# The last merge-gate units as Strassen pairs, and three helper chains cut into steps on VectorE's queue

## The chip, the cores and the metric

The kernel runs on one core of a Trainium2 chip. The number judged is the device time of one execution, in microseconds, the median over the runs of a kernel. Before the change it is 1549.16 us, the median of three runs that lie between 1545.98 and 1551.1 us. A separate execution was taken with the profiler; its own time was 1545.69 us and its span, from the first to the last recorded instruction, 1543.9 us.

The engines are TensorE (PE in the profile, with its weight loads as PEld), VectorE (DVE), ScalarE (ACT), GpSimd (POOL) and SyncE (SP), which here issues nearly all DMA transfers.

## What is computed

An encoder block over 1024 tokens of width 1024. A normalised input `h` is multiplied by one wide matrix; three attention branches (A, dilated windows in three groups; B, grouped-query; M, cross-attention into a memory) produce `oa`, `ob` and `om`, each 512 wide. What matters here is the end of it:

```python
h = rms_norm(x, g_pre[layer])
a_qkv, bq, bk, bv, mq, ga, gb, gm, mg = jnp.split(h @ w_in[layer], split_at, axis=-1)
...
wts = jax.nn.softmax(jnp.stack(lses, axis=0), axis=0).astype(dt)
oa = jnp.einsum('gbsh,gbshd->bshd', wts, jnp.stack(outs, axis=0)).reshape(b, s, BRANCH_WIDTH)
...
ya = (oa * jax.nn.silu(ga)) @ w_br_a[layer]
yb = (ob * jax.nn.silu(gb)) @ w_br_b[layer]
ym = (om * jax.nn.silu(gm)) @ w_br_m[layer]
gates = jax.nn.sigmoid((mg + b_merge[layer]).astype(jnp.float32)).astype(dt).reshape(b, s, N_BRANCHES, d)
merged = gates[:, :, 0] * ya + gates[:, :, 1] * yb + gates[:, :, 2] * ym
out = merged @ w_out[layer]
x = x + rms_norm(out, g_post[layer])
```

The merge gates `mg` are 3072 columns of the wide product: 24 units of 128 columns, each a product of 1024 x 128 weights with 1024 x 1024 of `h`.

## The kernel before

Everything is held transposed, channels on the 128 partitions and tokens along the row. Every float32 operand is split in two parts of a shorter type, high and low (`split`, lines 104 to 106: ScalarE copies to the high part, VectorE subtracts it to get the low part), and a product is three passes: high with high, high with low, low with high. `hh[k]` and `hl[k]` are the parts of `h`, k from 0 to 7.

`dense` (lines 139 to 148) does one half (512 tokens) of a unit of 128 output columns: 8 values of k times 3 passes, 24 matmuls of 128x512. A unit is 48 matmuls. `add_unit` queues such units with a function that takes each half out of PSUM; `weave` interleaves the queue's matmuls with an attention's, by costs. TensorE runs in the order written; the other engines' queues are ordered when the program is built, by a scheduler that looks at priorities and at when it thinks operands are there. A queue is strictly in order once built: what waits at its head holds up all behind it.

The stages, in the order of time: start and memory projection; branch M; branch B; branch A with twelve attentions (four pairs of heads p_, three groups g); the merge; the output projection. Ten of the 24 merge-gate units are computed early, as fillers during B and A (`add_filler`, `FILL_B`, `FILL_A`): the eviction multiplies by the row `rb` on VectorE (line 212), ScalarE does the tanh, and the result goes out to DRAM (`thd`).

`combine(p_, ogs)` (lines 1042 to 1072) is the softmax over the three groups of one pair of heads. It reads the statistics back, makes three weights per token on small tiles, writes them out, and then for each group and each half loads them broadcast over the partitions (`wgt`, line 1065, one buffer), multiplies (line 1069, VectorE, 128x512, read with a stride) and adds the groups on GpSimd (line 1071). For p_ = 0, 1, 2 it stands between two attentions; for p_ = 3 in the merge, behind the first branch's operands.

The merge (lines 1094 to 1192) goes over the branches in the order 2, 1, 0 and over eight column blocks f. `mg_unit` computes one merge gate (48 matmuls, for the 14 units that were not spilled) or loads it from `thd`; `y_unit` computes one block of a branch's product (24 matmuls), multiplies it by the gate on VectorE and adds it into `accs[f]` on GpSimd (line 1128). The gate runs two steps ahead of the product. A branch's operand is `od[i]` times its silu gate `g2d[i]` (and a normaliser for branch 1), split in parts; `g_load` fetches and multiplies, all of it in one place half way through the branch before. After the last product the eight weight tiles of the output projection are loaded and split (lines 1198 to 1203), and eight token blocks are projected, normalised and stored.

Of the kernel before, what the change touches and what calls it, by code (L numbers as in the profile page):

```python
# [8 lines left out]
F32 = mybir.dt.float32  # L9
R = mybir.dt.float32r  # L10
# [6 lines left out]
NT = 8  # L17
# [33 lines left out]
def block(ctx: ExitStack, tc: tile.TileContext, x, xT, memT, cst, msk, bcst, tabA, gpost,  # L51
# [757 lines left out]
    with tc.tile_pool(name="aa", bufs=1, reuse_waits="tile") as aa:  # L809
# [81 lines left out]
        def a_att(p_, g):  # L891
# [29 lines left out]
            st = {}  # L921
# [5 lines left out]
            def scores(T):  # L927
# [6 lines left out]
                for h in range(2):  # L934
# [4 lines left out]
                    V.tensor_tensor_reduce(raw, sv[:, h], mask[:, mo:mo + n], 1.0, 3.0e38, OP.add, OP.min, bias)  # L939
# [102 lines left out]
        def combine(p_, ogs):  # L1042
            cpt = cb.tile([P, 3, 2, 16], F32, name="cpt", bufs=1)
            for h in range(2):
                nc.sync.dma_start(cpt[h * 64:h * 64 + 64], std[p_, h].rearrange("g s (i e) -> i g s e", e=16))
            mn = cb.tile([P, 16], F32, name="cmn", bufs=2)
            V.tensor_tensor(mn, cpt[:, 0, 0], cpt[:, 1, 0], op=OP.min)
            V.tensor_tensor(mn, mn, cpt[:, 2, 0], op=OP.min)
            eg = cb.tile([P, 3, 16], F32, name="ceg", bufs=1)
            V.tensor_tensor(eg, cpt[:, :, 0], mn[:, None, :].to_broadcast([P, 3, 16]), op=OP.subtract)  # L1050
            A.activation(eg, eg, AF.Exp, scale=-1.0)
            dn = cb.tile([P, 3, 16], F32, name="cdn", bufs=1)
            V.tensor_tensor(dn, eg, cpt[:, :, 1], op=OP.mult)
            ds_ = cb.tile([P, 16], F32, name="cds", bufs=2)
            V.tensor_tensor(ds_, dn[:, 0], dn[:, 1], op=OP.add)
            V.tensor_tensor(ds_, ds_, dn[:, 2], op=OP.add)
            V.reciprocal(ds_, ds_)
            V.tensor_tensor(eg, eg, ds_[:, None, :].to_broadcast([P, 3, 16]), op=OP.mult)
            for h in range(2):
                nc.sync.dma_start(wgd[p_, h].rearrange("g (i e) -> i g e", e=16), eg[h * 64:h * 64 + 64])  # L1060
            for g in range(3):
                for e in range(2):
                    wgt = cb.tile([P, 512], F32, name="wgt", bufs=1)
                    for h in range(2):
                        nc.sync.dma_start(wgt[h * 64:h * 64 + 64],
                                          wgd[p_, h, g:g + 1, e * 512:e * 512 + 512].to_broadcast([64, 512]))
                    wv = wgt.rearrange("p (b a) -> p a b", b=8)
                    ogv = ogs[g].rearrange("p (a b) -> p a b", b=16)[:, :, e * 8:e * 8 + 8]
                    V.tensor_tensor(ogv, ogv, wv, op=OP.mult)
                if g:  # L1070
                    G.tensor_tensor(ogs[0], ogs[0], ogs[g], op=OP.add)
            nc.sync.dma_start(od[0, p_], ogs[0])

        seq = [(p_, g) for p_ in range(4) for g in range(3)]
# [3 lines left out]
        for n, (p_, g) in enumerate(seq):  # L1078
# [9 lines left out]
            if g == 2 and p_ < 3:  # L1088
                combine(p_, [OG.pop((p_, x)) for x in range(3)])

    end_psum()
# [3 lines left out]
    with tc.tile_pool(name="mg", bufs=1, reuse_waits="tile") as mg:  # L1095
        accs = [None] * 8
        extra.extend((mg, wp))

        def mg_unit(i, f):
            th = mg.tile([P, S], F32, name="th", bufs=3)  # L1100
            if 8 * i + f in spilled:
                nc.sync.dma_start(th, thd[8 * i + f])
                return th
            w = load_w(wu[U_M + 8 * i + f])
            s = pss()
            for half in range(2):
                for _ in dense(w, half, s[:, half]):
                    pass
            V.tensor_tensor(th, s.rearrange("p a b -> p (a b)"), rb, op=OP.mult)
            A.activation(th, th, AF.Tanh, scale=0.5, bias=hbm[:, 8 * i + f:8 * i + f + 1])  # L1110
            return th

        def y_unit(n, i, f, th, gh, gl):
            wh, wl = load_w(wbr[i, f], 512)
            s = pss()
            for half in range(2):
                t = slice(half * 512, half * 512 + 512)
                terms = []
                for k in range(4):
                    terms += [(wh[:, k, :], gh[k][:, t]), (wh[:, k, :], gl[k][:, t]), (wl[:, k, :], gh[k][:, t])]  # L1120
                passes(s[:, half], terms)
            sv = s.rearrange("p a b -> p (a b)")
            if n == 0:
                accs[f] = mg.tile([P, S], F32, name=f"acc{f}")
                V.scalar_tensor_tensor(accs[f], th, 1.0, sv, op0=OP.add, op1=OP.mult)
            else:
                V.scalar_tensor_tensor(th, th, 1.0, sv, op0=OP.add, op1=OP.mult)  # L1127
                G.tensor_tensor(accs[f], accs[f], th, op=OP.add)  # L1128

        def g_load(i):  # L1130
            ots = []
            for k in range(4):
                ot = (pre or mg).tile([P, S], F32, name="ot", bufs=4 if pre else 2)
                nc.sync.dma_start(ot, od[i, k])
                gt = mg.tile([P, S], F32, name="gt", tag="wr", bufs=2)
                nc.sync.dma_start(gt, g2d[i, k])
                V.scalar_tensor_tensor(ot, ot, 0.5, gt, op0=OP.mult, op1=OP.mult)
                if i == 1:
                    gt = mg.tile([P, S], F32, name="gt", tag="wr", bufs=2)
                    for h in range(2):  # L1140
                        nc.sync.dma_start(gt[h * 64:h * 64 + 64], rld[2 * k + h:2 * k + h + 1].to_broadcast([64, S]))
                    V.tensor_tensor(ot, ot, gt, op=OP.mult)
                ots.append(ot)
            return ots

        def g_split(ots):
            gh, gl = [], []
            for k, ot in enumerate(ots):
                a = mg.tile([P, S], R, name=f"gh{k}")
                b = mg.tile([P, S], R, name=f"gl{k}")  # L1150
                split(a, b, ot)
                gh.append(a)
                gl.append(b)
            return gh, gl

        def g_prep(i):
            gh, gl = [], []
            for k in range(4):
                ot = mg.tile([P, S], F32, name="ot", bufs=2)
                nc.sync.dma_start(ot, od[i, k])  # L1160
                gt = mg.tile([P, S], F32, name="gt", tag="wr", bufs=2)
                nc.sync.dma_start(gt, g2d[i, k])
                V.scalar_tensor_tensor(ot, ot, 0.5, gt, op0=OP.mult, op1=OP.mult)
                a = mg.tile([P, S], R, name=f"gh{k}")
                b = mg.tile([P, S], R, name=f"gl{k}")
                split(a, b, ot)
                gh.append(a)
                gl.append(b)
            return gh, gl

        pre = None
        steps = [(n, i, f) for n, i in enumerate((2, 1, 0)) for f in range(8)]
        ths = {}
        for m in range(len(steps) + 2):
            if m < len(steps):
                n, i, f = steps[m]
                ths[m] = mg_unit(i, f)
            if m >= 2:
                n, i, f = steps[m - 2]
                if f == 0:  # L1180
                    if n == 0:
                        gg = g_prep(i)
                        combine(3, [OG.pop((3, x)) for x in range(3)])
                        close(cbp)
                        prep, pre = pool("pre", "right")
                    else:
                        gg = g_split(ots)
                if f == G_AT and n < 2:
                    ots = g_load(1 - n)
                y_unit(n, i, f, ths.pop(m - 2), *gg)  # L1190

        close(prep)
# [187 lines left out]
```

## Time and profile before

| what | us |
|---|---|
| median of three runs | 1549.16 |
| the profiled execution, its own time | 1545.69 |
| its span | 1543.9 |
| start to the first attention of A | about 640 |
| twelve attentions of A, the last statistics transposed at | 1162.84 |
| merge, until the output projection's weights | about 1160 to 1432 |
| output projection and store | about 1432 to 1544 |

The statistics of the twelve attentions are transposed on TensorE (line 1016) at 659.59, 705.39, 746.61, 797.45, 843.26, 884.47, 936.71, 982.50, 1023.73, 1075.84, 1121.63 and 1162.84 us. The steps between them are 45.8 and 41.2 us for groups 1 and 2 in each pair of heads, and 50.8, 52.2 and 52.1 us for group 0 of pairs 1, 2 and 3, which follow a `combine`.

How to read it: a row of groups gives line, engine, operation, result and operands with their shapes, the count, the total and the mean duration, and then the time that the engine sat idle just before these instructions and what ended it. Matmuls overlap in the pipeline, so a matmul's duration is not its cost: the distance between two starts is.

### The profile page before, as it was taken

Reading aid. Unit: us, or ns where it says so; the run is one execution under the profiler, and the core shown is the slowest. Engines: PE = TensorE matmul, PEld = TensorE weight load, DVE = VectorE, ACT = ScalarE, POOL = GpSimd, SP = SyncE. Lnnn points to the kernel's source line nnn. Section 1 sums busy time; section 2 is a strip of 40 time slices with the busy share of each in tenths; the row PEclk is TensorE's granted clock in tenths of the full one; section 3 lists DMA queues with packets and bytes.
Section 4 is the critical chain, followed back from the end, with each engine's and each line's share of the span. In section 5 each row is a group of like instructions: output and inputs, shape, how many; then the busy total and the mean of one; then the engine's idle time right before and its main releaser. Section 6 shows DMA issues by size and latency. Waiting matters only on the chain.

```text
span 1543.9 us, 20861 instructions
## 1 busy us (share of the span) xinstructions
PE 1497.0 (97%) x7748; PEld 1237.3 (80%) x7748; DVE 977.3 (63%) x1610; ACT 712.1 (46%) x1457; POOL 443.4 (29%) x363
## 2 busy tenths in 40 slices
PE   6999989999999999999999999999999999999998
PEld 5899977777777778888878877887888788888787
DVE  7765469989988975655566566556634442524743
ACT  5443345666677661645545445454643111212321
POOL 4415513454444543211231222123100100222422
PEclk9999999999999999999999999999999999999999
DMA  5342011111111112111120121112125451523432
GB/s 210 96 124 69 29 45 59 54 56 48 62 35 59 62 64 88 38 28 42 58 69 29 42 72 55 42 34 84 37 69 186 149 159 34 193 80 113 126 110 96
DMA packets 56966, 119.81 MB, mean 78 GB/s; under 512 B 14176, under 2 KB 24096, under 8 KB 56736
## 3 DMA queue, kind: packets, MB, share of 16 engines
q1 hardware_dynamic: 56720, 118.34, 23.8%
q8 instruction: 61, 1.00, 0.3%
q14 instruction: 41, 0.34, 0.1%
q10 hardware_dynamic: 144, 0.13, 0.0%
HBM read 96.06 MB, written 22.38 MB: 77 GB/s over the span
## 4 chain that ended last, share of the span: by engine, by line
PE 74%; DVE 12%; DMA 4%; issue 4%; ACT 3%; POOL 2%; SPq 1%; DVEq 0%; POOLq 0%; ACTq 0%
PE d L147 12%; PE d L143 12%; PE d L145 12%; PE sc L125 7%; PE sc L1226 4%; PE s L125 3%; PE sc L147 2%; PE sc L145 2%; PE sc L143 2%; PE ov L989 2%; DMA wgt<-wgd 2%; DVE bpl L106 2%; PE s L709 1%; PE ov L730 1%; PE s L708 1%
## 5 line engine op out<-in xcount | busy, mean ns | idle before, releaser
L143 PE MATMUL d<-hh,wh 128*128 128x512 f32 x992 | 396.0, 399 | 2.4 <-DVE fth L222 2.4
L147 PE MATMUL d<-hh,wl 128*128 128x512 f32 x992 | 397.3, 400 | 0.0
L145 PE MATMUL d<-hl,wh 128*128 128x512 f32 x992 | 393.6, 397 | 0.0
L143 PEld LDWEIGHTS d<-hh,wh 128*128 128x128 f32 x992 | 187.2, 189 | 39.2 <-DVE fth L222 3.2
L147 PEld LDWEIGHTS d<-hh,wl 128*128 128x128 f32 x992 | 187.1, 189 | 39.0 <-issue 4.1
L145 PEld LDWEIGHTS d<-hl,wh 128*128 128x128 f32 x992 | 187.3, 189 | 36.2 <-issue 1.0
L105 ACT ACTIVATE wh<-wr 128x1024 fp32r<-128x1024 f32 (+1 forms) x100 | 95.4, 954 | 242.9 <-PE sc L145 107.6
L838 POOL TENSOR_TENSOR rot<-rot,t2a 128x512 f32<-128x512 f32 x48 | 82.6, 1720 | 313.6 <-DVE t2a L837 313.6
L720 POOL TENSOR_TENSOR bl<-bl,bp 128x512 f32<-128x512 f32 x96 | 135.5, 1412 | 120.4 <-ACT bp L711 112.0
L106 DVE TENSOR_TENSOR bpl<-bp,bph 128x512 fp32r<-128x512 f32 x128 | 130.5, 1020 | 23.8 <-ACT bph L105 23.3
L106 DVE TENSOR_TENSOR wl<-wr,wh 128x1024 fp32r<-128x1024 f32 (+1 forms) x100 | 120.7, 1208 | 21.9 <-ACT wh L105 21.2
L711 ACT ACTIVATE bp<-s 128x512 f32<-128x512 f32 x128 | 76.2, 595 | 60.0 <-PE s L709 58.1
L1128 POOL TENSOR_TENSOR acc<-acc,th 128x1024 f32<-128x1024 f32 x16 | 45.4, 2836 | 192.7 <-DVE th L1127 192.7
L947 ACT ACTIVATE pra<-pra,sts 128x128 f32<-128x128 f32 (+2 forms) x152 | 67.1, 442 | 61.3 <-DVE sts L939 60.6
L147 PE MATMUL sc<-hh,wl 128*128 128x512 f32 x224 | 87.3, 390 | 2.3 <-DVE wl L106 2.3
L691 DVE TENSOR_REDUCE bn<-tr 128x1 f32<-128x512 f32 x128 | 86.6, 680 | 4.4 <-PE tr L690 4.0
L939 DVE CUSTOM_DVE_ANT_0 pra<-s,mask 128x128 f32<-128x128 f32 (+2 forms) x152 | 48.3, 348 | 62.3 <-PE s L125 50.1
L143 PE MATMUL sc<-hh,wh 128*128 128x512 f32 x224 | 87.3, 390 | 0.0
L145 PE MATMUL sc<-hl,wh 128*128 128x512 f32 x224 | 87.1, 389 | 0.0
L105 ACT ACTIVATE bph<-bp 128x512 fp32r<-128x512 f32 x128 | 80.8, 631 | 3.5
L835 DVE TENSOR_TENSOR rot<-d,tab 128x512 f32<-128x512 f32 x48 | 33.1, 690 | 73.3 <-PE d L147 73.1
L125 PE MATMUL sc<-gh,wh 128*128 128x512 f32 x192 | 74.7, 389 | 0.0
(278 smaller groups left out, 3097.2 us busy)
## 6 DMA issues: line engine op xcount, KB each, us to landing
wr<-in_wu SPq DMA_DIRECT2D x76, 512.0 KB
g2d<-fth SPq DMA_DIRECT2D x24, 256.0 KB
wgt<-wgd SPq DMA_DIRECT2D x48, 128.0 KB
ot<-od SPq DMA_DIRECT2D x12, 512.0 KB
gt<-g2d SPq DMA_DIRECT2D x12, 512.0 KB
wr<-in_wbr SPq DMA_DIRECT2D x24, 256.0 KB
thd<-fth SPq DMA_DIRECT2D x20, 256.0 KB
th<-thd SPq DMA_DIRECT2D x10, 512.0 KB
```

Of the source, the lines that this page charges most:

```text
L105: A.activation(dst_h, src, AF.Copy)
L106: V.tensor_tensor(dst_l, src, dst_h.bitcast(F32), op=OP.subtract)
L125: PE.matmul(out_ps, a, b, start=i == 0, stop=i == n - 1)
L143: PE.matmul(dst, wh[:, k, :], hh[k][:, t], start=k == 0, stop=False)
L145: PE.matmul(dst, wh[:, k, :], hl[k][:, t], start=False, stop=False)
L147: PE.matmul(dst, wl[:, k, :], hh[k][:, t], start=False, stop=k == 7)
L691: V.tensor_reduce(st[i]["n"][:, j, c:c + 1], s, axis=AX.X, op=OP.min)
L711: A.activation(pp, s, AF.Exp, scale=-1.0)
L720: G.tensor_tensor(lsum[i % 2], lsum[i % 2], pp, op=OP.add)
L838: G.tensor_tensor(o[:, t], o[:, t], t2, op=OP.add)
L947: A.activation(src, raw, AF.Exp, scale=-1.0, bias=bias, accum_out=sts[:, h, 1, T:T + 1])
L1226: PE.matmul(parts[h], *terms[h][j], start=j == 0, stop=j == 23)
```

## The change

Three things.

First, `combine` and the loading of a branch's operands become lists of small functions. Each is called inside `tc.issue_after(instruction)`, which places what it issues behind that instruction on the instruction's queue: for the pairs of heads 0 to 2 behind the mask operation of scores T = 0, 2, 4, 6 of the next attention and T = 1 of the one after (`STEP_T`); for pair 3 behind evictions of filler units; for branch operands behind evictions in the merge. `combine` now loads and multiplies a group's 1024 tokens at once.

Second, of the 14 merge-gate units that were computed in the merge, four (`BRIDGE`) are now fillers in a stretch of their own after the last attention. The other ten are computed in five pairs by the Winograd form of Strassen's algorithm. Two units are the two block rows of a matrix, the halves of k its block columns; `h` is cut by halves of k and of tokens. Seven products of 12 matmuls each take the place of eight. The sums of `h` (T1 to T4) are made once, during the four fillers (`token_sums`: two VectorE adds per k to rejoin the parts, four GpSimd subtractions, three splits; T4 is split into the place of `hh[k]` and `hl[k]`, upper tokens, once the fillers are done). The sums of weights (S1 to S4) are made per pair (`wino_prep`: four GpSimd operations of 128x512, six splits). All gates go out to `thd`.

Third, the merge is now only the 24 `y_unit`s, in the branch order 1, 2, 0, all gates read from `thd`; branch operands are split into the places of `hh` and `hl`, and the output projection's weights are loaded and split during the last branch.

```diff
-            V.tensor_tensor(th, p, rb[:, half * 512:half * 512 + 512], op=OP.mult)
+            fp["last"] = V.tensor_tensor(th, p, rb[:, half * 512:half * 512 + 512], op=OP.mult)
...
-                    yield scores(T)
+                    cost = scores(T)
+                    if todo and T == STEP_T[-len(todo)]:
+                        with tc.issue_after(last["dve"].ins):
+                            todo.pop(0)()
+                    yield cost
...
+            def load(g):
+                wgt[g] = cb.tile([P, S], F32, name="wgt", bufs=1)
+                for h in range(2):
+                    nc.sync.dma_start(wgt[g][h * 64:h * 64 + 64], wgd[p_, h, g:g + 1].to_broadcast([64, S]))
...
+            def weigh(g):
+                wv = wgt[g].rearrange("p (b a) -> p a b", b=16)
+                ogv = ogs[g].rearrange("p (a b) -> p a b", b=16)
+                V.tensor_tensor(ogv, ogv, wv, op=OP.mult)
+                if g < 2:
+                    load(g + 1)
+                if g:
+                    G.tensor_tensor(ogs[0], ogs[0], ogs[g], op=OP.add)
+                if g == 2:
+                    nc.sync.dma_start(od[0, p_], ogs[0])
+
+            return [fetch, weights] + [lambda g=g: weigh(g) for g in range(3)]
+
+        todo = []
+        STEP_T = (0, 2, 4, 6, 1)
...
+    def token_sums(k):
+        xs = []
+        for i in (k, k + 4):
+            xa = tb.tile([P, S], F32, name="xa" if i < 4 else "xb", bufs=2)
+            V.tensor_tensor(xa, hh[i].bitcast(F32), hl[i].bitcast(F32), op=OP.add)
+            xs.append(xa)
...
+        for n, dst, u, v in (("T1", t1, b12, b11), ("T2", t2, b22, t1), ("T3", t3, b22, b12)):
+            G.tensor_tensor(dst, u, v, op=OP.subtract)
+            split(*TB[n][k], dst)
+        G.tensor_tensor(t4[k], b21, t2, op=OP.subtract)
+
+    def tail():
+        com = combine(3, [OG.pop((3, x)) for x in range(3)])
+        for k in range(5):
+            if k:
+                with tc.issue_after(fp["last"].ins):
+                    com.pop(0)()
+            else:
+                com.pop(0)()
+            yield 1.0
+            if k < 4:
+                token_sums(k)
+                yield 1.0
...
+    for j in later[:BRIDGE]:
+        add_filler(j)
+    weave(BRIDGE, tail(), 10.0, 1.0, 0)
+    later = later[BRIDGE:]
+    for k in range(4):
+        split(*TB["T4"][k], t4[k])
...
+    def wino_prep(src1, src2):
+        r1 = wp.tile([P, 1024], F32, name="wr", bufs=WR)
+        r2 = wp.tile([P, 1024], F32, name="wr", bufs=WR)
+        nc.sync.dma_start(r1, src1)
+        nc.sync.dma_start(r2, src2)
...
+        split(wh, wl, r1)
...
+        G.tensor_tensor(s1, a21, a22, op=OP.add)
+        G.tensor_tensor(s2, s1, a11, op=OP.subtract)
+        G.tensor_tensor(s3, a11, a21, op=OP.subtract)
+        G.tensor_tensor(s4, a12, s2, op=OP.subtract)
+        out = {"A11": (wh[:, lo_t], wl[:, lo_t]), "A12": (wh[:, hi_t], wl[:, hi_t])}
+        for n, v in (("S2", s2), ("S3", s3), ("A22", a22), ("S1", s1), ("S4", s4)):
+            out[n] = (sr.tile([P, 512], R, name="ch", bufs=5), sr.tile([P, 512], R, name="cl", bufs=5))
+            split(*out[n], v)
+        return out
...
+        def out(u, t, E, x, y):
+            r = tmp("rs", 3)
+            E.tensor_tensor(r, x, y, op=OP.add)
+            ins = V.tensor_tensor(r, r, rb[:, hi_t if t else lo_t], op=OP.mult)
+            evac(u, t, r)
+            return ins
...
+        A.activation(p1, prod("A11", "B11"), AF.Copy)
+        step(V.tensor_tensor(v, prod("S2", "T2"), p1, op=OP.add))
+        step(out(0, 0, V, prod("A12", "B21"), p1))
+        step(V.tensor_tensor(y, prod("S3", "T3"), v, op=OP.add))
+        step(out(1, 0, V, prod("A22", "T4"), y))
+        A.activation(p5, prod("S1", "T1"), AF.Copy)
+        G.tensor_tensor(w, v, p5, op=OP.add)
+        step(out(1, 1, G, y, p5))
+        step(out(0, 1, V, prod("S4", "B22"), w))
...
+    steps = [(n, i, f) for n, i in enumerate((1, 2, 0)) for f in range(8)]
...
+        ins = y_unit(n, f, *nxt.pop(0), gg)
+        if n < 2:
+            if f == 0:
+                todo_g = g_load(2 - 2 * n)
+            if f < 6:
+                with tc.issue_after(ins.ins):
+                    todo_g.pop(0)()
...
+        else:
+            wo_load(f)
...
+BRIDGE = 4
```

More of the change, by code (lines that the diff above doesn't have):

```diff
@@ L920, in a_att @@
             sts = cb.tile([P, 2, 2, NT], F32, name="sts", bufs=2)
-            st = {}
+            st, last = {}, {}
             def blocks_of(T):
@@ L938, in scores @@
                     raw = sv[:, h] if moved else src
-                    V.tensor_tensor_reduce(raw, sv[:, h], mask[:, mo:mo + n], 1.0, 3.0e38, OP.add, OP.min, bias)
+                    last["dve"] = V.tensor_tensor_reduce(raw, sv[:, h], mask[:, mo:mo + n], 1.0, 3.0e38, OP.add, OP.min, bias)
                     if moved:
@@ L1042, in combine @@
         def combine(p_, ogs):
[L1043 to L1069, printed above, removed]
+            c = {}
@@ new lines, in tail @@
+    def tail():
[10 more added lines that the diff above has]
+                yield 1.0
+    later = [8 * i + f for i in (2, 1, 0) for f in range(8) if 8 * i + f not in spilled]
+    fp["p"] = tb
+    for j in later[:BRIDGE]:
+        add_filler(j)
@@ new lines, in block, with g_load, load, first @@
+    hooks, ots = [], []
+    def g_load(i):
+        ots.clear()
+        steps, last = [], {}
+        def load(k, what):
+            last["g"] = pre.tile([P, S], F32, name="gt", bufs=1)
+            if what:
+                nc.sync.dma_start(last["g"], g2d[i, k])
+            else:
+                for h in range(2):
+                    nc.sync.dma_start(last["g"][h * 64:h * 64 + 64],
+                                      rld[2 * k + h:2 * k + h + 1].to_broadcast([64, S]))
+        def first(k):
+            ot = pre.tile([P, S], F32, name="ot", bufs=4)
+            nc.sync.dma_start(ot, od[i, k])
+            ots.append(ot)
+            load(k, True)
+        def gate(k):
+            V.scalar_tensor_tensor(ots[k], ots[k], 0.5, last["g"], op0=OP.mult, op1=OP.mult)
+            if i == 1:
+                load(k, False)
+            elif k < 3:
+                first(k + 1)
+        def norm(k):
+            V.tensor_tensor(ots[k], ots[k], last["g"], op=OP.mult)
+            if k < 3:
+                first(k + 1)
+        steps.append(lambda: first(0))
+        for k in range(4):
+            steps += [None] * 1 + [lambda k=k: gate(k)]
+            if i == 1:
+                steps += [None] * 1 + [lambda k=k: norm(k)]
+        return [s or (lambda: None) for s in steps]
@@ new lines, in block, with y_load, y_unit @@
+    mgp, mg = pool("mg", "right")
+    myp, my = pool("my")
+    accs = [None] * 8
+    wo = [(hh[k + 4], hl[k + 4]) for k in range(4)]
+    def y_load(i, f):
+        th = my.tile([P, S], F32, name="th", bufs=3)
+        nc.sync.dma_start(th, thd[8 * i + f])
+        return load_w(wbr[i, f], 512), th
+    def y_unit(n, f, w, th, gg):
+        wh, wl = w
+        s = pss()
+        for half in range(2):
+            t = slice(half * 512, half * 512 + 512)
+            terms = []
+            for k in range(4):
+                gh, gl = gg[k]
+                terms += [(wh[:, k, :], gh[:, t]), (wh[:, k, :], gl[:, t]), (wl[:, k, :], gh[:, t])]
+            passes(s[:, half], terms)
+        sv = s.rearrange("p a b -> p (a b)")
+        if n == 0:
+            accs[f] = mg.tile([P, S], F32, name=f"acc{f}")
+            return V.scalar_tensor_tensor(accs[f], th, 1.0, sv, op0=OP.add, op1=OP.mult)
+        ins = V.scalar_tensor_tensor(th, th, 1.0, sv, op0=OP.add, op1=OP.mult)
+        G.tensor_tensor(accs[f], accs[f], th, op=OP.add)
+        return ins
@@ new lines, in wo_load @@
+    def wo_load(k):
+        raw = my.tile([P, D], F32, name="gt", bufs=2)
+        nc.sync.dma_start(raw, wout[k])
+        split(*wo[k], raw)
+    steps = [(n, i, f) for n, i in enumerate((1, 2, 0)) for f in range(8)]
+    for hook in hooks:
+        hook()
+    gg = g_split(ots, 0)
+    nxt = [y_load(*steps[0][1:])]
+    extra.extend((my, wp))
+    nxt.append(y_load(*steps[1][1:]))
+    for m, (n, i, f) in enumerate(steps):
+        if m + 2 < len(steps):
+            nxt.append(y_load(*steps[m + 2][1:]))
+        ins = y_unit(n, f, *nxt.pop(0), gg)
[3 more added lines that the diff above has]
+            if f < 6:
+                with tc.issue_after(ins.ins):
+                    todo_g.pop(0)()
+                    if f % 2:
+                        todo_g.pop(0)()
+            if f == 7:
+                assert not todo_g
+                gg = g_split(ots, 4 - 4 * n)
+                if n == 1:
+                    wo += [(mg.tile([P, D], R, name=f"woh{k}"), mg.tile([P, D], R, name=f"wol{k}")) for k in range(4, 8)]
+        else:
+            wo_load(f)
```

280 lines of the change are left out of this document (133 added, 147 removed).

## The prediction

> **What bounds the kernel now.** I read the page's busy table first, then the waits of TensorE, then the chain of waits, then stretches of the timeline and windows around the longest waits.
>
> ```profile
> PE 1497.0 (97%) x7748; PEld 1237.3 (80%) x7748; DVE 977.3 (63%) x1610; ACT 712.1 (46%) x1457; POOL 443.4 (29%) x363
> ...
> PE tr L965 <- ACT app L977: 10.4, 3, 3.6
> PE sc L147 <- DVE wl L106: 2.3, 1, 2.3
> PE sc L1226 <- DVE wol L106: 1.1, 1, 1.1
> ...
> 1328.92 32.64 PE sc L125 x144
> ```
>
> The first line is the busy table: TensorE is busy 97% of the span. The next three, from the waits, are what it still waited for behind the first attention: three waits of about 3.5 us each at the first transposes after a `combine`, one of 2.3 us in the merge, one of 1.1 us at the output projection. The last, from the chain, gives the price of a matmul: 144 of 128x512 in 32.64 us, 0.2267 us from start to start (each one's 0.39 us overlaps the next). So the end is set by the number of matmuls plus a few waits.
>
> Two more views decide this forecast. The timeline (start, duration) at 1395 us, and at the 2.3 us wait:
>
> ```profile
> 1395.57 5.68 DVE L106 TENSOR_TENSOR gl<-ot,gh 128x1024 fp32r<-128x1024 f32 x3
> ...
> 1395.73 3.30 POOL L1128 TENSOR_TENSOR acc<-acc,th 128x1024 f32<-128x1024 f32 x1 [13.74 <-DVE th L1127]
> ...
> 1216.76 2.38 POOL L1071 TENSOR_TENSOR og<-og 128x1024 f32<-128x1024 f32 x1 [7.59 <-DVE og L1069]
> ...
> 1217.64 2.58 DVE L106 TENSOR_TENSOR wl<-wr,wh 128x1024 fp32r<-128x1024 f32 x1
> ```
>
> Three splits that take 1.21 us each alone need 5.68 us together when a GpSimd addition of 2.39 us falls between them, and that addition takes 3.30; at 1217.64 a split ends only 1.1 us after GpSimd's addition has ended (1219.14). A VectorE operation with two operands in SBUF and a GpSimd operation on tensors exclude each other: they run one after the other, though on two engines. Evictions with an operand in PSUM do not take part (L212 keeps 0.68 us under GpSimd). So for such work the sum over both engines counts, not each alone.
>
> **What goes.** Matmuls: 5 pairs x 12 x 0.2267 = 13.6 us. The three waits behind `combine`: 787.10 to 790.81, 924.97 to 928.96 and 1064.21 to 1068.1 (10.9 us above the normal step). They come from VectorE standing in its queue for the chain wgt load, multiplication, next load (2.9 to 3.1 us a load in the chain of waits); in steps two scores apart (about 4 us each) a load has 8 us, so I take all of it. After two of the three the clock falls:
>
> ```profile
> 788.00:792.00 4.00, 1.19 (x8) 0.78 (x8) 3.07 (x5) 4.00 (x9) 0.00 (x0) 1.00 0.38 134
> ...
> 929.00:933.00 4.00, 4.00 (x30) 3.25 (x32) 3.50 (x4) 2.84 (x3) 0.79 (x2) 0.57 0.02 5
> ...
> 1069.00:1073.00 4.00, 4.00 (x35) 3.52 (x34) 3.49 (x3) 2.04 (x4) 0.79 (x2) 0.57 0.00 0
> ```
>
> The third figure from the end of a window is the granted clock: 0.57 over 4 us is 3.4 us at half, which loses 1.7 us; twice, 3.4 us. That agrees with the group steps: 50.8, 52.2, 52.1 us after a `combine`. Bounds of this term: 10.4 (waits alone) to 14.8 (steps against 46.8); I take 14.3. The 2.4 us at 1217 and the 1.3 us at the output projection go too, since neither a gate unit nor a late weight split stands there any more: 3.7. Together 31.6 us.
>
> **What comes: the four fillers (the bridge).** In the built order VectorE and GpSimd must get through this between the start of the bridge and the first use of S2 in the second product of pair 0. Durations are starts apart in queues: two-operand 128x512 0.60 us (0.68 less the overlap), 128x1024 1.13, a strided 128x1024 twice 1.09 less overlap, 2.1; GpSimd 1.28 (smallest of L720 1.272, median 1.297) and 2.39.
> - VectorE, two SBUF operands: 8 rejoining adds 9.0, 12 splits of T1 to T3 7.2, 4 weight splits 4.5, 3 weighings 6.3, seven small steps of `weights` 1.0, 4 splits of T4 2.4, one of S2 0.6: 31.0.
> - GpSimd: 16 subtractions 20.5, 2 additions of the groups 4.8, S1, S3 and S2 (they stand behind these additions in its queue) 3.8: 29.1.
>
> 60.1 us that exclude each other. They can't start before the second filler's weights are split, 1.2 us in, since that split waits for the last A filler's matmuls to free its buffer and stands ahead of the first rejoining add. The second product is due 4 x 10.88 + 2.72 = 46.2 us in. So TensorE loses at least about 14.5 us. Walking the queues with the rows' durations (ready requests served in turn), TensorE stops for the eviction of the second, third and fifth half (3.9, 1.2 and 3.8 us: an eviction stands behind a split that waits for a GpSimd subtraction; two banks) and for the sixth (0.4), and 9.0 us for S2: the third weighing waits for its load (issued behind the second; 4.4 us for 512 KB as at `wr<-in_wout`), then the addition, S1, S3, S2 alternate with four splits of T4, and ScalarE makes S2's high part only behind the tanh of the last eviction. Sum 18.2. I take 18, between 13 (all handoffs overlapping by 0.1 us) and 22 (loads slow, wrong partner served first). Clock after the 9 us wait: 1.7 us at half rate, bounds 0 and 3.4.
>
> The Trainium skill, "TensorE: Matmul & The Clock Gate", section "What's actually happening", has the array back at half rate after an idle window of about 3.4 us. The trace agrees for 3.8 and 3.6 us of wait and shows 1.00 after the 3.5 at 787. By that rule the bridge's 3.9 and 3.8 us would cost 1.7 us each on top; the sum would be 3.4 us higher if TensorE and not VectorE set the pace there.
>
> **The five pairs.** TensorE needs 84 x 0.2267 = 19.04 us a pair. Work that excludes each other, for a pair in the middle: GpSimd 6 x 1.28, VectorE 5 + 4 x 0.60 and 1.13 for weights, 8 multiplications of branch operands over three pairs 3.0: 17.2 us, 90%. Raw tiles are a loop: four sums (5.1) must be done before the next pair's first load starts (0.5 + 4.4), ScalarE's split (1.06) holds up six operations of 0.6 to 0.72 up to the eviction of the sixth product (4), then GpSimd's two operations (2.6) go ahead of the next sums: 17.6 us, with a VectorE operation ahead of each GpSimd one 21.2. That is about TensorE's pace, and the first load of pair 1 has some 10 us to spare. I take 1.5 us, bounds 0 and 7.
>
> **The merge without gates.** A `y_unit` each 24 x 0.2267 = 5.44 us. VectorE's eviction 1.22, splits 0.68 + 1.2; GpSimd's addition 2.4: what excludes each other is 4.2 of 5.44. Loads: 768 KB of gate and weights and on average 512 KB of operands per 5.44 us, 240 GB/s, where a window of 10 to 20 us after the start moved 405. Gates are three buffers deep: a load takes about 5 us and is needed 16 us after the release. Start: the operands of branch 1 are split into `hh[0..3]` only after product 5 of the last pair, 5.4 us before its end; four splits with GpSimd between, 8 us, first needed in steps of 0.68: 0.7 us late. I take 0.7, bounds 0 and 5.
>
> **Steps in the attentions.** Each weighing (2.2 us) stands behind the scores' mask on VectorE, the next scores' mask and exp behind it, transposes two scores later: 8 us of cover. SP holds weight loads behind a `wgt` that waits for a weighing: weights are loaded a unit (10.9 us) ahead. I take 0.5, bounds 0 and 4; without the cover each of 9 waits would be some 2 us.
>
> **Sum.** 1545.7 (profiled execution) - 31.6 + 18 + 1.7 + 1.5 + 0.7 + 0.5 = 1536.5. The median of the runs lies 3.5 us above that execution: 1540.
>
> **Rivals.**
> - The bridge hides its work: if the exclusion cost nothing, VectorE alone has 31 + 5.5 (evictions) in 46 us and only the chain behind the last weighing is late, 2 to 3 us: 1549.2 - 31.6 + 2.5 + 3 = 1523. For it: 63% VectorE on average. Against: the two timelines above. 0.12.
> - The pairs become the bound (slower): the raw-tile loop misses at each hop, because branch operands (2 MB that start just before pair 1's loads, 5 us at 405 GB/s, and 0.5 MB a step later) go ahead on SP and in the engines: 21.2 + 5 = 26 against 19.04, over three loops 21 us: 1540 + 20 = 1560. For it: SP's order has the operand loads ahead, ScalarE's and VectorE's splits of coming weights stand ahead of evictions. Against: ten us of head start, loads of 4.4 us. It decides from a loop of 22 us on. 0.18.
> - The steps don't do what they say: `wgt` still comes late, and VectorE waits behind the scores as before: the 14.3 us stay, 1554. For it: the same number of transfers in series. Against: 8 us of room. 0.1.
>
> **Chances and range.** The forecast 0.6, its own range 1531 to 1550. A change of 0.3%, 4.6 us, is about what a measurement here can tell from none: faster is below 1544.5. Of the forecast's 0.6 some 0.47 lies there, 0.12 within and 0.01 above; the first rival adds 0.12 to faster, the second 0.18 to slower, the third 0.05 to each of within and slower. Faster 0.59, within 0.17, slower 0.24. The range takes in the lower part between forecast and first rival and the upper bounds of the bridge and the pairs: 1526 to 1557.
>
> **What would show it.** After: 60 matmuls fewer; no wait `tr <- app` of over 3 us, group 0 steps near 47 us; GpSimd and VectorE durations in the bridge stretched over their own (subtractions well over 1.28, splits over 0.68), TensorE's waits in the bridge and before S2 some 18 us, the last behind an `L105`/`L106` split of S2; pairs 19 to 20 us apart; `y_unit`s 5.44 us apart. Wrong if the bridge shows under 8 us of waits, or if a pair takes over 21 us.

## The result, and the profile after

The changed kernel takes 1556.43 us (median of 7 runs, 1553.44 to 1557.69), the kernel before in the same comparison 1547.5 (7 runs, 1544.43 to 1551.1). The ratio is 1.0056, interval 1.0041 to 1.0071: slower, by more than the 0.3% that can be told from none. The forecast was 1540, faster. The profiled execution took 1554.28 us, 17.8 more than the 1536.5 of the sum, its span 1552.5.

The busy table of the changed kernel:

```profile
PE 1492.1 (96%) x7688; PEld 1227.5 (79%) x7688; DVE 1056.1 (68%) x1681; ACT 737.4 (47%) x1517; POOL 516.2 (33%) x409
```

60 matmuls are gone, TensorE's busy time fell by 4.9 us, and the span is 8.6 us longer: TensorE waits more. The waits of TensorE (engine, line, for whom; total, times, longest, in us):

```profile
PE s L125 <- ACT ch L105: 7.8, 1, 7.8
...
PE d L143 <- DVE fth L212: 5.1, 2, 2.9
...
PE s L125 <- DVE rs L1202: 4.3, 1, 4.3
...
PE sc L125 <- DVE wl L106: 3.9, 5, 1.7
PE sc L125 <- ACT wh L105: 3.6, 2, 2.5
...
PE tr L965 <- ACT app L977: 1.5, 3, 0.6
```

The last row was 10.4 us before: the steps of `combine` did what they say. The five above it are new, and each belongs to one place: the first use of S2, the bridge's evictions, a product of the fourth pair that waits for its PSUM bank, and the low and high parts of the merge's weights.

The account, by the statistics transposes and TensorE's starts: up to the first statistics 1.0 us more; over the attentions 11.0 less; from the last statistics to the start of the last matmul 18.5 more (393.2 for 374.7). These 18.5 are 13.6 less for matmuls, 22.8 more for waits above 0.5 us (26.5 for 3.7), 3.2 more for small ones, and 5.9 for matmuls at half clock, where there were none before: 18.3.

How the longest wait comes about is in the timeline of VectorE and GpSimd (start, duration):

```profile
1203.83 0.68 DVE L212 TENSOR_TENSOR fth<-d,rb 128x512 f32<-128x512 f32 x1
1204.43 7.58 DVE L106 TENSOR_TENSOR hl<-tb,hh 128x512 fp32r<-128x512 f32 x4
...
1204.05 2.40 POOL L1087 TENSOR_TENSOR og<-og 128x1024 f32<-128x1024 f32 x1 [4.19 <-DVE og L1083]
1206.42 1.70 POOL L1179 TENSOR_TENSOR sf<-wr 128x512 f32<-128x512 f32 x1
1208.08 1.70 POOL L1181 TENSOR_TENSOR sf<-wr 128x512 f32<-128x512 f32 x1
1209.75 1.71 POOL L1180 TENSOR_TENSOR sf<-sf,wr 128x512 f32<-128x512 f32 x1
```

Four splits of T4 (0.68 us each alone) take 7.58 in all, the last three GpSimd operations (1.28 each alone) some 1.70 each: the two engines take turns, the first split behind GpSimd's addition. S2 (line 1180) is done at 1211.46, and ScalarE begins its high part at 1213.79, behind the tanh of the last eviction (1212.69) and a copy; TensorE had asked at 1206.25. So the last 2.3 us of this wait are ScalarE's order, not the turns. The same in the fourth pair, between 1283 and 1289:

```profile
1283.19 1.76 DVE L1203 TENSOR_TENSOR rs<-rs,rb 128x512 f32<-128x512 f32 x1 [2.44 <-POOL rs L1202]
1284.87 2.29 DVE L1246 SCALAR_TENSOR_TENSOR ot<-ot,gt 128x1024 f32<-128x1024 f32 x1
1287.08 1.75 DVE L106 TENSOR_TENSOR cl<-sf,ch 128x512 fp32r<-128x512 f32 x1
1288.75 0.68 DVE L1202 TENSOR_TENSOR rs<-s,ww 128x512 f32<-128x512 f32 x1
...
1284.36 1.72 POOL L1181 TENSOR_TENSOR sf<-wr 128x512 f32<-128x512 f32 x1
1286.04 2.24 POOL L1180 TENSOR_TENSOR sf<-sf,wr 128x512 f32<-128x512 f32 x1
```

The eviction that frees the bank (1288.75) takes no turns (0.68 us), but it stands behind three operations that do: 0.60, 1.13 and 0.60 apart alone, they take 5.6 us, and TensorE stops for 4.5.

In the merge, the longest of the five waits for a weight's low part (1.7 us, from 1407.50 on) goes back to such a turn too:

```profile
1401.56 2.77 POOL L1316 TENSOR_TENSOR acc<-acc,th 128x1024 f32<-128x1024 f32 x1 [4.65 <-DVE th L1315]
...
1402.43 2.99 DVE L1246 SCALAR_TENSOR_TENSOR ot<-ot,gt 128x1024 f32<-128x1024 f32 x1 [0.34 <-DMA gt<-g2d]
1406.54 1.23 DVE L106 TENSOR_TENSOR hl<-ot,hh 128x1024 fp32r<-128x1024 f32 x1 [1.13 <-ACT hh L105]
1407.68 1.22 DVE L1315 SCALAR_TENSOR_TENSOR th<-th,sc 128x1024 f32<-128x1024 f32 x1
1408.82 0.69 DVE L106 TENSOR_TENSOR wl<-wr,wh 128x512 fp32r<-128x512 f32 x1
```

The multiplication of a branch operand takes 2.99 us beside GpSimd's addition and ends 1.1 us after it (1.22 us in all, in the run that has the additions on VectorE). The weight's low part (`wl`), itself only 0.69 us, stands behind what follows from it: the operand's split and an eviction.

### The profile page after: what moved, and what is told of

Read it like the earlier page. It is cut to its first block, busy times and chain, and to the rows that moved or that the text cites. A ratio compares the mean times of both kernels' runs of the same rounds, so it can differ in the third digit from the quotient of the medians.

```text
span 1552.5 us, 21074 instructions
## 1 busy us (share of the span) xinstructions
PE 1492.1 (96%) x7688; PEld 1227.5 (79%) x7688; DVE 1056.1 (68%) x1681; ACT 737.4 (47%) x1517; POOL 516.2 (33%) x409
## 4 chain that ended last, share of the span: by engine, by line
PE 64%; DVE 14%; issue 9%; POOL 5%; ACT 4%; DMA 4%; SPq 0%; DVEq 0%; POOLq 0%; ACTq 0%
PE d L147 12%; PE d L143 12%; PE d L145 12%; PE sc L125 5%; PE sc L1378 4%; PE s L125 3%; DVE bpl L106 2%; PE ov L989 2%; DVE bn L691 2%; PE d L537 1%; PE s L709 1%; PE s L708 1%; PE ov L730 1%; PE ov L729 1%; DVE wl L106 1%
## 5 line engine op out<-in xcount | busy, mean ns | idle before, releaser
L143 PE MATMUL d<-hh,wh 128*128 128x512 f32 x1056 | 421.6, 399 | 7.4 <-DVE fth L212 5.1
L147 PE MATMUL d<-hh,wl 128*128 128x512 f32 x1056 | 422.4, 400 | 0.0
L145 PE MATMUL d<-hl,wh 128*128 128x512 f32 x1056 | 419.2, 397 | 0.0
L143 PEld LDWEIGHTS d<-hh,wh 128*128 128x128 f32 x1056 | 199.5, 189 | 47.6 <-ACT T1h L105 3.3
L147 PEld LDWEIGHTS d<-hh,wl 128*128 128x128 f32 x1056 | 199.4, 189 | 41.3 <-issue 3.7
L145 PEld LDWEIGHTS d<-hl,wh 128*128 128x128 f32 x1056 | 199.4, 189 | 38.7 <-issue 1.0
L106 DVE TENSOR_TENSOR bpl<-bp,bph 128x512 fp32r<-128x512 f32 x128 | 131.7, 1029 | 23.8 <-ACT bph L105 23.3
L106 DVE TENSOR_TENSOR wl<-wr,wh 128x1024 fp32r<-128x1024 f32 (+1 forms) x95 | 114.6, 1207 | 33.1 <-ACT wh L105 32.4
L125 PE MATMUL sc<-hh,wl 128*128 128x512 f32 x192 | 75.5, 393 | 3.9 <-DVE wl L106 3.9
L125 PE MATMUL sc<-hh,wh 128*128 128x512 f32 x192 | 75.0, 391 | 3.6 <-ACT wh L105 3.6
L125 PE MATMUL sc<-hl,wh 128*128 128x512 f32 x192 | 74.9, 390 | 0.0
L862 ACT ACTIVATE akh<-rot,cs 128x1024 fp32r<-128x1024 f32 x24 | 43.1, 1799 | 44.8 <-POOL rot L838 35.9
```

What stands on the lines that cost most here:

```text
L106: V.tensor_tensor(dst_l, src, dst_h.bitcast(F32), op=OP.subtract)
L125: PE.matmul(out_ps, a, b, start=i == 0, stop=i == n - 1)
L143: PE.matmul(dst, wh[:, k, :], hh[k][:, t], start=k == 0, stop=False)
L145: PE.matmul(dst, wh[:, k, :], hl[k][:, t], start=False, stop=False)
L147: PE.matmul(dst, wl[:, k, :], hh[k][:, t], start=False, stop=k == 7)
```

## The experiments

Each ratio is against runs of the kernel before on the same chip. Unless said otherwise an edit is made in the changed kernel.

**The subtractions of `token_sums` on VectorE.**

```diff
-            G.tensor_tensor(dst, u, v, op=OP.subtract)
+            V.tensor_tensor(dst, u, v, op=OP.subtract)
...
-        G.tensor_tensor(t4[k], b21, t2, op=OP.subtract)
+        V.tensor_tensor(t4[k], b21, t2, op=OP.subtract)
```

> The changed kernel with the sixteen subtractions of the bridge (T1 to T4) on VectorE instead of GpSimd; nothing else. Theory A (VectorE and GpSimd exclude each other, so the bridge is as long as the sum of both engines' work): 16 x 1.28 us become 16 x 0.60, the sum falls from 60 to 49 us, TensorE's waits in the bridge and before S2 fall from 13.4 us to 3 or less, and the stretches at half clock behind them (3.4 and 10.2 us long, 6.8 us lost at most) go: 1538 to 1544. Theory B (VectorE's own queue and the chain of wgt loads set it): VectorE's 36 us grow by 9.6 and fill the 46 us, the waits stay or grow: 1556 or more.

1552.14 us, ratio 1.0024 (1.0008 to 1.0040): 4 us better, between the two. The bridge's wait of 3.0 us went, but the built order now had the first pair's weights behind the T4 splits, and these still took turns with GpSimd's S1 to S4:

```profile
1198.10 7.55 DVE L106 TENSOR_TENSOR hl<-tb,hh 128x512 fp32r<-128x512 f32 x4
1205.58 0.68 DVE L212 TENSOR_TENSOR fth<-d,rb 128x512 f32<-128x512 f32 x1
1206.18 1.68 DVE L106 TENSOR_TENSOR wl<-wr,wh 128x1024 fp32r<-128x1024 f32 x1
```

TensorE waited 9.6 us for that `wl` in place of 8.0 for S2.

**The steps alone.** The kernel before, with `combine` for pairs 0 to 2 in steps, its 1024 tokens loaded at once as in the change, and nothing else:

```diff
-                combine(p_, [OG.pop((p_, x)) for x in range(3)])
+                todo += combine(p_, [OG.pop((p_, x)) for x in range(3)])
```

> The kernel before with combine of pairs 0 to 2 in steps behind the scores, the whole 1024 tokens at once; merge, gates and branch operands as before (combine of pair 3 called in one piece). If the steps are worth what the changed kernel shows between the first and the last attention, 10 us: 1537 to 1539 against 1547.5. Rival (what is saved there is lost again in the merge, because the merge waits for something else): 1545 or more.

1537.06 us, ratio 0.9922 (0.990 to 0.9945). This third of the change is worth some 11 to 12 us (10.9 by the spans of the two traces, 11.6 by the medians); no stretch at half clock is left in the attentions. The other two thirds together therefore cost some 19 us, though they save 60 matmuls.

**Six units as fillers, four pairs** (`BRIDGE = 6`).

> The changed kernel with six fillers in the bridge and four Strassen pairs: 12 matmuls more, 2.7 us. Theory A (amount of excluding work against the length of the bridge): 60 us against 68, so the 8.0 us wait before S2 and the 10.2 us at half clock behind it (5.1 us lost) go, the 5.4 us inside the bridge stay: 1545 to 1549. Theory B (the wait for S2 hangs on the chain behind the last weighing, whenever that is): the wait stays and 2.7 us are added: 1557 to 1560.

1554.08 us, ratio 1.0032 (1.0019 to 1.0045): in neither range. The wait for S2 went to 1.4 us as theory A has it, but others grew. Inside the bridge 10.6 us are lost where theory A kept 5.4, the longest 6.1 for an eviction that stands behind a weighing of 2.96 us (2.0 where GpSimd doesn't hold it up). And 3.9 us come at the merge's start, for a bank: ScalarE's copy that frees it stands behind four copies of branch operands (1.04 to 1.05 us each) and a tanh, and no GpSimd operation runs there. So more time helps little while the engines take turns, and not all that is lost is turns.

**The merge's accumulation on VectorE.**

```diff
-        G.tensor_tensor(accs[f], accs[f], th, op=OP.add)
+        V.tensor_tensor(accs[f], accs[f], th, op=OP.add)
```

> The changed kernel with the accumulation of the merge on VectorE instead of GpSimd. Theory A: a weight split of 0.68 us waits behind GpSimd's 2.4 us additions; on VectorE an addition takes 1.13 us, the five waits for wl between 1407 and 1441 (5.4 us) go: 1550 to 1552. Theory B (the loads of weights are late there): 1555 or more.

1550.19 us, ratio 1.0010 (0.9999 to 1.0022). Theory A: the row `PE sc L125 <- DVE wl L106` is gone, so the five waits for a weight's low part in the merge hang on the addition being on GpSimd. The splits themselves took 0.7 us in the changed kernel; how each came to be late was followed for the longest alone, above. What is left there is one wait of 3.9 us at the merge's start, for a weight load that SP issues late.

**All sums of the operands on VectorE**: the subtractions of the first experiment, and S1 to S4 too.

> As the sums on VectorE before, and the four sums of weights per pair (S1 to S4) on VectorE too, so that GpSimd does only the two additions of combine in the bridge and two operations per pair. Theory A (exclusion): the four splits of T4 no longer take turns with S1 to S4 (1.74 us each, 0.6 alone), the wait for A11's low part falls from 9.6 us to 2 or 3, its half-clock stretch goes, the wait of 2.2 us for a bank in pair 3 goes: 1540 to 1545. Theory B (the chain of three wgt loads ends the bridge): the third weighing ends where it did, the wait stays over 7 us: 1549 or more.

1540.05 us, ratio 0.9953 (0.9938 to 0.9968): theory A. No wait in the last four pairs is left, each takes 19.04 us; 5.9 us (2 or 3 had been expected) and 1.4 at the first pair and the waits for `wl` in the merge remain.

**Nothing of pairs and merge on GpSimd**: the last one, with the sums `w` and `out(1, 1)` of a pair and the accumulation on VectorE.

> As the run with all sums on VectorE, and also the last two GpSimd operations of a pair and the accumulation of the merge on VectorE. Theory A: the merge's waits for wl (5 us) and what is left in the pairs go as well: 1535 to 1540. Theory B (VectorE now has too much of its own): slower than the run with all sums on VectorE.

1530.79 us, ratio 0.9898 (0.9881 to 0.9914), 25.6 us below the changed kernel and more than theory A asked for. Past 1160 us TensorE waits only for 1.6 (an eviction), 5.9 (low part of A11) and 1.4 (S2).

**TensorE kept busy ahead of S2.** 32 matmuls are added between the first and second product of pair 0, into a bank that nobody reads, to keep the clock up where the 8 us wait is.

> The changed kernel with 32 more matmuls of 128x512 (7.3 us) between the first and the second product of pair 0, into a bank that nobody reads: TensorE works through most of the 8.0 us in which it waits for S2. Theory C (the half-clock stretch of 10.2 us behind that wait costs 5.1 us of its own): no such stretch there, and 4 to 5 us less: 1551 to 1552.5. Rival (VectorE sets the pace there and the slow clock is hidden): 1555 or more.

1557.5 us, ratio 1.0066 (1.0051 to 1.0081): the rival. No wait and no half clock are left at S2, and pair 0 takes 26.3 us, 7.3 of it the added matmuls, for 29.6. But the next pairs, 19.0, 19.0, 26.1 and 19.0 us in the changed kernel, take 19.9, 24.1, 24.0 and 19.0:

```profile
PE s L125 <- DVE rs L1204: 6.7, 2, 3.4
PE d L143 <- DVE fth L212: 6.4, 3, 3.1
```

The first row (waits of TensorE) is the eviction of line 1202 in this kernel's numbering, now late twice. So with GpSimd in the loop what is gained ahead of the pairs is lost in them: there the queues of VectorE and GpSimd set the pace of those that run over 19.04 us.

**The first pair's weights ahead of T4.** From here on the base is the kernel without GpSimd (1530.79). `wino_prep` is cut in two, and its loads and first split are issued ahead of the T4 splits:

```diff
+    ready = wino_load(wu[U_M + pairs[0][0]], wu[U_M + pairs[0][1]])
     for k in range(4):
         split(*TB["T4"][k], t4[k])
```

> The kernel with nothing of the end left on GpSimd (1530.79), but the weights of the first pair are split ahead of the four splits of T4, which the fourth product alone needs. There TensorE waited 5.93 us for the low part of A11 and 1.41 us for S2, and ran 6.8 us at half clock after it. Theory A (that wait is the place where the end is still set): the low part comes 4 us earlier, S2's chain of three operations and a split then ends about 2.5 us late: waits of 3 to 4 us in place of 7.3, half of the lost clock regained: 1523 to 1528. Rival (the pairs behind it are paced by VectorE's queue, so that what is gained at their start is lost before the merge, as with the filled wait): 1529 to 1532.

1529.74 us, ratio 0.9877 (0.9862 to 0.9892): hardly less, in the rival's band, but not for the rival's reason. Every later pair takes 19.04 us. The two waits shrank from 7.3 to 5.0 us, and half clock rose from 6.8 to 10.2 us of time, which cost 3.4 in place of 1.6. What is left of the first wait is again exclusion, with GpSimd's addition of the last group:

```profile
1189.53 5.66 POOL L1087 TENSOR_TENSOR og<-og 128x1024 f32<-128x1024 f32 x1 [87.79 <-issue]
1199.07 2.36 POOL L1087 TENSOR_TENSOR og<-og 128x1024 f32<-128x1024 f32 x1 [3.88 <-DVE og L1083]
...
1199.42 3.09 DVE L106 TENSOR_TENSOR wl<-wr,wh 128x1024 fp32r<-128x1024 f32 x1
```

**Those two additions on VectorE too**, in the last kernel (line 1087, `G` to `V`).

> The last kernel with four fillers and the two additions of the groups of the last pair of heads on VectorE, the only GpSimd work left there. In it the split of the first pair's weights takes 3.09 us beside such an addition of 2.36 (alone 1.21), and the addition before it stretches to 5.66. Theory A (the exclusion): the split takes 1.21 us, the wait for A11's low part goes from 2.94 to about 1 us, and with it part of the half clock: 1525 to 1528.5. Rival (VectorE has no room for 2.3 us more in its queue): the waits stay and the time is 1529.5 to 1532.

1533.03 us, ratio 0.9910 (0.9893 to 0.9926): above both ranges. But line 1087 also serves the `combine` of the first three pairs of heads, so the edit changes the attentions too, and the stages have to be read apart. From the first to the last statistics the trace is 3.3 us longer than before this edit (496.25 for 492.96: each step of group 0 behind a `combine` 0.7 to 0.8 us more, each next step 0.3 to 0.4). From the last statistics on it is 1.5 us shorter (374.71 for 376.21): the split takes 1.21 us and the wait for A11 goes, as theory A has it, but an eviction comes 2.8 us late and S2 3.2, with all of it in VectorE's queue. The whole time therefore doesn't decide between the two; the last pair's two additions alone were not moved.

**Six fillers again, now without GpSimd** (`BRIDGE = 6` in the kernel with the weights ahead of T4).

> The last kernel (1529.74, weights of the first pair ahead of T4) with six units as fillers and four pairs: 12 matmuls more, 2.7 us, and 21.8 us more of TensorE's time over VectorE's work on the sums. Left there are waits of 1.61, 2.94 and 2.06 us and 10.2 us at half clock, up to 11.7 us in all. Theory A (the start of the pairs is the last place where the freed kernel loses): the waits and the half clock go and the time is 1521 to 1526. Rival (a pair is paced by VectorE and not by TensorE, so that the wait at its start is regained there): only the 2.7 us show, 1530 to 1533.

1523.53 us, ratio 0.9849 (0.9835 to 0.9864): theory A, and the fastest of all. Its busy table, and the waits of TensorE on the lines of the change:

```profile
PE 1485.9 (98%) x7700; PEld 1227.1 (81%) x7700; DVE 1043.7 (69%) x1728; ACT 736.5 (48%) x1511; POOL 401.5 (26%) x347
```

```profile
PE tr L965 <- ACT app L977: 1.6, 3, 0.6
PE s L125 <- ACT ch L105: 1.2, 1, 1.2
```

Twelve matmuls more than in the changed kernel, and 33 us less. `BRIDGE = 6` is worth 4 to 6 us here (0.0028 by the ratios, 6.2 by the medians), and was worth 2 to 4 with GpSimd taking turns (0.0024 and 2.3).

**The steps alone, with the accumulation on VectorE.** It is the yardstick for the rest of the change, Strassen and the new merge together: the merge of before, with as little on GpSimd.

> The kernel before with the steps of combine alone (1537.06, two waits of 2.78 and 0.95 us left in its merge), its merge's accumulation moved from GpSimd to VectorE. It gives the kernel without Strassen under the same freedom from exclusion as the best one. Theory A (what Strassen is worth is the difference to 1530.79, and the two waits are of a weight split behind a GpSimd addition): 1533 to 1535.5, so Strassen with its sums on VectorE is worth 2 to 5 us of its 13.6. Rival (the two waits have another cause): 1536.5 to 1538, worth 6 to 7 us.

1533.35 us, ratio 0.9907 (0.9886 to 0.9927): theory A. The wait for `wl` in its merge fell from 2.8 to 1.2 us. The kernel with five pairs and nothing on GpSimd but the group additions (0.9877) gains only 0.3% on it, within the intervals; the one with four pairs (0.9849) gains 0.6%, some 9 us, of the 10.9 that its 48 matmuls are worth (4 x 12 x 0.2267).

## Why the prediction was wrong

**The mechanism of the bridge was right, and it was not carried through the rest.** VectorE operations with two operands in SBUF and GpSimd operations exclude each other, and this is most of what the change dies of: with the same matmuls and the same arithmetic, moving GpSimd's part of it to VectorE gives 25.6 us. The Trainium skill, "SBUF — State Buffer", section "SBUF: two separate sides", says that GpSimd and a VectorE operation with two inputs in SBUF hold a shared pair of ports in turn, each for a whole instruction; the 7.58 us for four splits and the 1.70 us of the GpSimd operations between them agree.

**What held.** Matmuls: 13.6, three of the five pairs at 19.04 us. The two waits in merge and output projection: gone, 3.7. The two timelines of before were enough to find the places: `fth` in the bridge, then S2.

**What was mis-sized**, from the last statistics on (the prediction had 4.6 us more in this part, and it became 18.5):

| term | predicted | measured |
|---|---|---|
| bridge and S2, waits | 18 | 13.4 |
| half clock | 1.7 | 5.9 |
| the five pairs, wait | 1.5 | 4.5 |
| the merge, waits | 0.7 | 8.6 |
| small waits | 0 | 3.2 |

- **The merge** is the step that failed most: 0.7 us was put where 8.6 came. The prediction put its exclusive work at 4.2 of 5.44 us per `y_unit` and took only its start as late. That sum has no place for the multiplications of branch operands, and a sum below the pace isn't enough anyway: an operation that comes beside an addition of 2.4 to 2.8 us waits for its end, as the one of 2.99 us above did, and the weight splits that stand behind have no slack for that. With the addition on VectorE these waits (5.9 us) went. The other 2.7 us are a weight load at the merge's start, which SP issues at 1325.04 us, behind two stores of the last pair's gates, 8.5 us after the merge's first matmul; TensorE waits from 1327.45 on. With S1 to S4 and the subtractions on VectorE the same load comes 5.8 us after it and there is no wait; how GpSimd's sums delay it is not shown.
- **The pairs.** The forecast chose its loop of 17.6 us (below 19.04) over the 21.2 with a VectorE operation ahead of each GpSimd one, and 1.5 us. The measured 4.5 us, and 2.3 to 2.6 at half clock behind it, are such an episode: it comes where the multiplication of branch operands (`ot`, 2.29 us) falls between. That is the rival's mechanism at a third of its price: that pair took 26.1 us, close to the rival's 26, but the rival asked for three such. It is also over the 21 us that the prediction had named as a sign of being wrong.
- **The bridge** was walked too slowly. Its first evictions cost 3.0 and 2.4 us for 3.9, 1.2, 3.8 and 0.4; S2's wait of 8.0 stands where 9.0 was put. Its least loss, 15.1 us by its own figures (1.2 + 60.1 - 46.2; it wrote 14.5), was not reached either.
- **The clock.** 1.7 us for one stretch; there were three, behind the waits of 3.0, 8.0 and 4.5 us. The prediction had named 3.4 us more for the bridge's shorter waits and left them out of its sum. The last section says by which rule the clock goes.
- **`combine`.** 14.3 was taken between 10.4 and 14.8, less 0.5 for the steps; the attentions became 11.0 shorter. A wait of 0.6 to 0.8 us stays at each of the three places.

The misses of the stage add up to 13.7 (4.2 + 3.0 + 7.9 + 3.2 - 4.6), `combine` to 2.8, the start to 1.0: 17.5 of the 17.8. That the bridge was put too dear was luck for the forecast: it hides 4.6 us of the other misses.

**Why moving work helps at all.** GpSimd needs 1.28 us for what VectorE does in 0.60, and 2.39 for 1.13. Where the two can't overlap, a GpSimd operation costs the pair of engines twice what it would cost VectorE: by the prediction's counts the bridge's 60.1 us become 31.0 + 16 x 0.60 + 3 x 0.60 + 2 x 2.39 = 47.2, against 46.2 until the second product. That fits the runs: the freed kernel still waited with four fillers, and no longer with six (21.8 us more). The sum is an estimate, and ScalarE's part in these waits is not in it.

## What to carry to other kernels

Where two engines exclude each other, count a GpSimd operation not as help but as VectorE's time at GpSimd's price, and move it to VectorE if that sum then fits. GpSimd may pay beside VectorE operations that read PSUM, which kept their 0.68 us here; no run tried to place its work there. A sum below TensorE's pace hides nothing by itself: look for the short operation that TensorE waits for and add to it one whole operation of the other engine for each that stands ahead of it. Work saved on TensorE is worth its time only if what replaces it fits in the cover there: against the steps alone, 60 matmuls less cost 19 us here, and 48 less, with a longer cover and the sums on VectorE, gave 9. And where an edited line serves two stages, read the stages apart before you believe the whole time.

## What the runs showed of the hardware

**The clock goes by fixed windows of 3.41 us, and by how busy TensorE was in the last one.** The changed kernel at the wait for S2, cut at that grid (stretch and its length, then busy time of PE, PEld, DVE, ACT and POOL with counts, granted clock, DMA share, GB/s):

```profile
1206.00:1209.40 3.40, 0.64 (x3) 0.19 (x1) 3.40 (x3) 0.36 (x1) 3.40 (x3) 1.00 0.60 231
1209.40:1212.80 3.40, 0.00 (x0) 0.00 (x0) 3.21 (x3) 0.11 (x1) 3.32 (x3) 0.50 0.41 154
1212.80:1216.20 3.40, 1.74 (x4) 1.41 (x5) 1.76 (x3) 3.40 (x7) 0.33 (x1) 0.50 0.56 182
1216.20:1219.60 3.40, 3.40 (x9) 2.63 (x9) 1.34 (x3) 0.29 (x1) 0.00 (x0) 0.50 0.95 354
1219.60:1223.00 3.40, 3.40 (x16) 2.79 (x16) 0.85 (x2) 1.06 (x1) 0.00 (x0) 1.00 1.02 414
```

A window with 0.64 us of matmuls is followed by half clock; one half busy leaves it there; a full one brings it back. This grid was laid over the thirteen traces, from the first change of the granted clock near 220 us on, and read from 230 to 1520 us; busy is the time with any matmul under way. From full clock, every window with TensorE busy for up to 42% was followed by half clock, and every one with 47% or more was not. From half clock, up to 76% it stayed, from 83% it rose. So the length of a wait doesn't decide alone: 3.5 us at 787 in the kernel before lies across two windows, each about half busy, and costs nothing, while 3.0 us at 1174 lies in one and costs 1.6. And two short waits in a row keep the clock down for 10.2 us, as with the first pair's weights ahead of T4.

The Trainium skill, "TensorE: Matmul & The Clock Gate", section "What's actually happening", has free-running windows of 3413 ns, the throttle after an idle one and release after a busy one. The grid agrees; idle here means under some 45% busy, and busy over some 80%.

**The two engines don't always take turns.** GpSimd's group addition of 5.66 us above started at 1189.53 and had to wait until 1192.86, when VectorE came to an eviction out of PSUM; four more two-operand operations went ahead of it (from 1192.86 it took the 2.36 of its like). It was GpSimd's first operation after 87.79 us of idling. At 1206 in the changed kernel VectorE and GpSimd changed after every operation. What decides this was not tried.
